# Sample attention in four column groups of TensorE, with plain float32 values

## The chip, the cores and the metric

The kernel runs on one core of a Trainium2 chip. The metric is the device time of one execution in microseconds (us). TensorE is PE in the profile (PEld are its weight loads), VectorE is DVE, ScalarE is ACT, GpSimd is POOL, and SP is the queue that issues the weight transfers.

## The reference

One layer of a hybrid decoder works on a prompt of 1024 tokens and on 8 samples of 4 new tokens each. It has a big input projection, a convolution branch with a LayerNorm, a state-space (S5) branch, dilated attention, an output projection and a feed-forward block. The change lies in the attention of the samples:

```python
kcat = concatenate([k_buf, k_new]);  vcat = concatenate([v_buf, v_new])
idx = L + j - kk * dil                      # 129 keys of each pattern
s = einsum('bthc,btkhc->bhtk', q, kcat[:, idx]) * ATT_SCALE + bias
mx = max(s);  p = exp(s - mx);  den = sum(p)
o = einsum('bhtk,btkhc->bthc', p, vcat[:, idx]) / den;  lse = mx + log(den)
att = sum(softmax(stack(lse over the 3 patterns)) * stack(o))
```

There are 3 patterns of 4 heads of 64. Weighting the three outputs by their denominators is the same as one softmax over the keys of all three patterns, and so the kernel treats them.

## The kernel before, in words

The main line is a list of atoms (`Atom`, run by `run`): dense matmuls `z<-hh,whi` and the like, each f32 product made of three float32r products of high and low halves (`gemm`), 24 matmuls of 128x352 for one chunk of one weight tile. Beside it side generators emit their instructions into the same engine queues: `Side.advance` counts the cost of each atom down, and a generator goes on when its last `yield` is used up. So the numbers after `yield` (`YL`, `YA` to `YD` at the top of the file) set where in each engine's order a step stands. PE, ACT, DVE and POOL work through their orders one instruction after the other.

While the gate projections run (`gate_jobs(GS, 0)`), two generators live beside them: `ln_gen` (L1555 to L1604), the LayerNorm of the convolution branch in three chunks, and `sample_gen` (L946 to L1083), the attention of the samples. `sample_gen` goes like this:

1. Queries go into `Qz`, 32 columns for each pattern, head pair p and sample, zero but for their own place (a memset and 24 copies, L956 and L969), and into `Qa` for the new keys.
2. Scores. `load_k` (L952, POOL) brings the 896 cached keys of one sample, 128x1792, into one of three buffers `kc`. In four bursts, one for each two samples, three key ranges (512, 128 and 256 keys) get four matmuls each: two samples by two head pairs. All four add into the same 32 rows of the score tile, `rows = slice(b2 * 32, b2 * 32 + 32)`. A row stands for sample, head and token.
3. `Qa` against the new keys, the table of biases (L993, L995), exp on ACT (L1016), division on DVE (L1019): tile `Ss`.
4. Ten transposes of `Ss` on PE (L1028, L1039); the 7 tiles of cached keys are split into high and low float32r halves (`PTs`, ACT L1032 and DVE).
5. Values. `load_v` (L1002) uses the buffers of `kc` again. `split_v` makes a high half on ACT (`vh`, L1010) and a low half on DVE (`vl`), in 16 half samples u; each of 56 tiles of 128 keys takes two matmuls into `so[0:32]`.
6. After each two samples ACT copies the sums (`Av`, L1061), four PE transposes turn them (L1067), and at the end the new values are added (`nw`, `asm`) and stored for the branch's projection.

A row block of 32 of a PSUM tile is fed by 32 of the 128 columns of PE's array; such a block is called a column group here. Helpers hide the lines: `mm` records all matmuls as L309 and `TT` all tensor_tensor as L312.

Of the kernel before, what the change touches and what calls it, by code (L numbers as in the profile page):

```python
# [8 lines left out]
F32 = mybir.dt.float32  # L9
# [43 lines left out]
C_ID, C_ONE = 0, 128  # L53
NCST = 256

# [201 lines left out]
def program(tc, I, O):  # L257
# [688 lines left out]
    def sample_gen():  # L946
# [6 lines left out]

        Qz = sa.tile([128, 1792], F32, tag="qp", name="Qz")[:, 0:1536]
        Qz = Qz.rearrange("p (g t b x) -> p g t b x", g=3, t=2, b=8)
        dve.memset(Qz, 0.0)  # L956
        for b in range(3):
# [3 lines left out]
        for g in range(3):  # L961
            for p in range(2):
                for h in range(2):
                    for par in range(2):
                        hp_ = slice(h * 64, h * 64 + 64)
                        c0 = par * 16 + (2 * p + h) * 4
                        dst = Qz[hp_, g, p].rearrange("p (b2 two) x -> p b2 two x", two=2)[:, :, par, c0:c0 + 4]
# [10 lines left out]
        for b2 in range(4):  # L978
            rows = slice(b2 * 32, b2 * 32 + 32)
            for g, c0, n in QK:  # L980
                o = sA[rows, 0:512] if g == 1 else sB[rows, c0 - 512:c0 - 512 + n]
# [15 lines left out]
        vts = {}  # L997
        vhs, vls = {}, {}
# [5 lines left out]
        def split_v(u):  # L1004
            if u < 16:
                b, ks = u // 2, slice(0, 4) if u % 2 == 0 else slice(4, 7)
                n = ks.stop - ks.start
                vhs[u] = sa.tile([128, 4, 256], F32R, tag="vh", name="vh", bufs=2)
                vls[u] = sa.tile([128, 4, 256], F32R, tag="vl", name="vl", bufs=2)
# [10 lines left out]
        yield YB  # L1020

        PTs = sa.tile([128, 7, 8, 2, 16], F32R, tag="qp", name="PTs")
        for half in range(2):
# [5 lines left out]
            for i in range(n):  # L1029
                sv = s[:, i * 128:(i + 1) * 128].rearrange("p (b x) -> p b x", b=8)  # L1030
                ph, pl = [PTs[:, half * 4 + i, :, w, :] for w in range(2)]
# [8 lines left out]
        act.activation(out=PTn.rearrange("p k x -> p (k x)"), in_=s[0:32, 0:384], func=AF.Copy)  # L1040
        split_v(0)
        split_v(1)
        yield 3.0
        Av = sa.tile([128, 1024], F32, tag="Ss", name="Av")
        sT = st()
        for u in range(16):
            b, k0 = u // 2, 4 * (u % 2)
            n = 4 - u % 2
            if u % 4 == 0:
                so = st()  # L1050
            cb = (b % 2) * 256
            for kt in range(n):
                w = PTs[:, k0 + kt].rearrange("p b w x -> p b (w x)")[:, b]
                mm(so[0:32, cb:cb + 256], w, vhs[u][:, kt], u % 2 == 0 and kt == 0, False)
                mm(so[0:32, cb:cb + 256], w, vls[u][:, kt], False, u % 2 == 1 and kt == n - 1)
            split_v(u + 2)
            if u % 2 and b + 3 < 8:
                load_v(b + 3)
            if u % 4 == 3:
                av = Av[0:32, (u // 4) % 2 * 512:(u // 4) % 2 * 512 + 512]  # L1060
                act.activation(out=av, in_=so[0:32, :], func=AF.Copy)  # L1061
            yield YD
            if u % 4 == 3:
                for b2 in range(2):
                    for p in range(2):
                        c0 = p * 256 + (b - 1 + b2) * 32
# [8 lines left out]
        for p in range(2):  # L1075
            for h in range(2):
                hp_ = slice(h * 64, h * 64 + 64)
                c0 = (2 * p + h) * 4
                o = asm[hp_, p, :].rearrange("p (b j) -> p b j", b=8)
                sv = sT[hp_, p * 256:(p + 1) * 256].rearrange("p (b x) -> p b x", b=8)  # L1080
# [1347 lines left out]
```

## Time and profile before

| | us |
|---|---|
| median of 3 runs (1953.93 to 1955.24) | 1955.16 |
| the profiled execution's own time | 1954.96 |
| its span, first to last instruction | 1953.2 |
| PE busy in the span | 1865.4 |
| DVE busy | 1328.9 |
| ACT busy | 727.0 |
| POOL busy | 230.7 |

The profile is one execution. A row of its groups gives an operation with its shape, how often it ran, its busy time and mean length, and the idle time of its engine just before it with what ended that. A plain float32 matmul (weights and values not float32r) leaves two records in the trace, so 48 matmuls of the scores are 96 records. A matmul's record runs on while the next has begun, so its cost in a stream is the distance from start to start.

### The profile page before, as it was taken

The page shows a single profiled execution, that of the slowest core. Times are in us where ns is not written, and L with a number is a line of the kernel's source. Part 1 is how long each engine was busy: PE and PEld are TensorE (multiplying, and loading weights), DVE is VectorE, ACT ScalarE, POOL GpSimd, SP SyncE. Part 2 cuts the span into 40 slices and gives each one's busy share as a digit, 9 for nine tenths or more (in the row PEclk, how much of TensorE's full clock was granted, in tenths as well). Part 3 has the DMA queues.
Part 4 walks back from the last instruction along what each step waited for, and adds up shares of the span by engine and source line. Part 5 has one row for each costly group of instructions (what it writes and reads, how often), then busy time and mean ns, then how long its engine had stood idle before and what let it go on. Part 6 is the DMA issues. An engine that isn't in the chain of part 4 may idle for free. (4 is left out here: it accounts for less than half of the span.)

```text
span 1953.2 us, 33675 instructions
## 1 busy us (share of the span) xinstructions
PE 1865.4 (96%) x13524; PEld 1747.0 (89%) x13524; DVE 1328.9 (68%) x2734; ACT 727.0 (37%) x1430; POOL 230.7 (12%) x386
## 2 busy tenths in 40 slices
PE   7999999899999899999899999999999999999995
PEld 2899799689787789999799999989999999999995
DVE  4777686366366667675596667777777777666695
ACT  3422432432432444222233445434333333374361
POOL 0000001001001013222200001100000000110024
PEclk9999999999999999999899999999999999999997
DMA  7333233233338444233842345542333223576663
GB/s 287 100 102 102 64 109 121 90 107 113 123 123 299 175 163 142 94 118 107 248 144 88 114 149 198 209 160 76 114 107 98 94 83 114 180 245 231 205 211 112
DMA packets 87550, 279.41 MB, mean 143 GB/s; under 512 B 15809, under 2 KB 21537, under 8 KB 85217
## 3 DMA queue, kind: packets, MB, share of 16 engines
q1 hardware_dynamic: 50096, 135.61, 21.7%
q0 software_dynamic: 29952, 115.17, 16.9%
q10 hardware_dynamic: 7344, 26.47, 4.0%
q8 instruction: 106, 1.74, 0.4%
q14 instruction: 52, 0.42, 0.1%
HBM read 209.98 MB, written 68.15 MB: 142 GB/s over the span
## 5 line engine op out<-in xcount | busy, mean ns | idle before, releaser
L309 PE MATMUL z<-hh,whi 128*128 128x352 f32 x1152 | 381.1, 331 | 2.8 <-ACT hh L649 1.5
L309 PE MATMUL z<-hh,wlo 128*128 128x352 f32 x1152 | 374.6, 325 | 3.1 <-DVE wlo L417 3.1
L309 PE MATMUL z<-hl,whi 128*128 128x352 f32 x1152 | 374.1, 325 | 0.8 <-DVE hl L312 0.8
L309 PE MATMUL z<-mh,wop 128*128 128x264 f32 x1916 | 369.4, 284 | 5.4 <-DVE wop L2055 3.0
L309 PE MATMUL z<-ml,wop 128*128 128x264 f32 x1300 | 317.6, 284 | 0.1
L309 PEld LDWEIGHTS z<-mh,wop 128*128 128x128 f32 x1916 | 305.4, 188 | 6.6 <-DVE wop L2055 3.8
L417 DVE SCALAR_TENSOR_TENSOR wlo<-raw,whi 128x1024 fp32r<-128x1024 f32 x132 | 160.9, 1222 | 131.9 <-ACT whi L416 125.1
L309 PEld LDWEIGHTS z<-hh,whi 128*128 128x128 f32 x1152 | 219.9, 191 | 13.9 <-issue 6.2
L309 PEld LDWEIGHTS z<-ml,wop 128*128 128x128 f32 x1300 | 224.1, 188 | 0.3 <-DVE ml L312 0.3
L309 PEld LDWEIGHTS z<-hh,wlo 128*128 128x128 f32 x1152 | 219.8, 191 | 3.7 <-DVE wlo L417 3.7
L309 PEld LDWEIGHTS z<-hl,whi 128*128 128x128 f32 x1152 | 220.1, 191 | 2.4 <-DVE hl L312 1.3
L416 ACT ACTIVATE whi<-raw 128x1024 fp32r<-128x1024 f32 x132 | 139.3, 1056 | 181.8 <-PE z L309 159.9
L1536 DVE SCALAR_TENSOR_TENSOR ycv<-cub,vecs,ycv 128x1024 f32<-128x1024 f32 x120 | 153.9, 1282 | 3.1
L2051 ACT ACTIVATE wop<-raw 128x512 fp32r<-128x512 f32 x132 | 80.7, 619 | 129.5 <-PE z L309 117.0
L309 PE MATMUL z<-xa,wop 128*128 128x264 f32 x768 | 103.7, 284 | 0.0
L309 PEld LDWEIGHTS z<-xa,wop 128*128 128x128 f32 x768 | 97.1, 188 | 0.1
L312 DVE TENSOR_TENSOR wop<-raw,wop 128x512 fp32r<-128x512 f32 x90 | 61.9, 689 | 44.5 <-ACT wop L2051 44.4
L309 PE MATMUL z<-mh,whi 128*128 128x264 f32 x288 | 85.8, 298 | 0.8 <-DVE ft L312 0.6
L309 PE MATMUL z<-ml,whi 128*128 128x264 f32 x288 | 83.3, 289 | 0.0
L309 PE MATMUL z<-mh,wlo 128*128 128x264 f32 x288 | 83.1, 289 | 0.0
L309 PE MATMUL z<-zh,whi 128*128 128x264 f32 x256 | 73.7, 288 | 0.0
L831 ACT ACTIVATE P<-P,stt 128x128 f32<-128x128 f32 (+1 forms) x96 | 42.1, 440 | 83.6 <-DVE stt L828 83.6
(462 smaller groups left out, 3780.2 us busy)
## 6 DMA issues: line engine op xcount, KB each, us to landing
raw<-i_win SPq DMA_DIRECT2D x48, 512.0 KB, 3.8
raw<-i_wfi SPq DMA_DIRECT2D x43, 512.0 KB, 4.0
raw<-i_wfo SPq DMA_DIRECT2D x72, 256.0 KB, 3.5
fd<-ft POOLq DMA_DIRECT2D x22, 792.0 KB, 6.8
raw<-i_wmod SPq DMA_DIRECT2D x32, 512.0 KB, 4.5
gd<-g ACTq DMA_DIRECT2D x24, 528.0 KB, 2.9
g<-gd ACTq DMA_DIRECT2D x24, 528.0 KB, 4.6
ml<-fd POOLq DMA_DIRECT2D x20, 528.0 KB, 6.6
```

What stands on the lines that cost most here:

```text
L309: return pe.matmul(out=out, lhsT=lhsT, rhs=rhs, start=start, stop=stop, **kw)
L312: dve.tensor_tensor(out=out, in0=a, in1=b, op=op)
L416: act.activation(out=hi[:, 0:n], in_=raw[:, 0:n], func=AF.Copy, scale=scale)
L417: dve.scalar_tensor_tensor(out=lo[:, 0:n], in0=raw[:, 0:n], scalar=scale, in1=hi[:, 0:n].bitcast(F32), op0=ALU.mult, op1=ALU.subtract)
L831: act.activation(out=P[:, h, 0:nk], in_=P[:, h, 0:nk], func=AF.Exp, scale=-1.0, bias=stt[:, b, hd:hd + 1], accum_out=stt[:, b, 4 + hd:5 + hd])
L1536: dve.scalar_tensor_tensor(out=a_, in0=ub[:, k:k + TP], scalar=wv[:, k:k + 1], in1=a_, op0=ALU.mult, op1=ALU.add)
L2051: act.activation(out=w[:, 0:n], in_=src, func=AF.Copy, scale=scale)
```

## The change

The scores get their rows in another order: head pair, then parity of the sample, then its number. Each of the four matmuls of two samples then has 32 rows of its own, and the four pairs of samples add into them. The key tiles of a sample's values go over four column groups too, as plain float32 products with unsplit values: four tiles at once, then three. The four partial sums are added while they are turned, by a product with a 128x16 matrix of ones and zeros (`C_FOLD`) in place of the transposes. The yields are new: 72 dense matmuls instead of 24 stand between the softmax and its transposes, a turn stands two steps behind the products it takes, and the LayerNorm's steps stand elsewhere among the dense work.

```diff
-YL = (5.0, 4.0, 4.28, 5.58)
-YA, YB, YC, YD = 4.443, 4.8, 3.45, 1.884
+YL = (5.0, 4.2, 3.8, 4.6)
+YA, YB, YC, YD, YE = 4.443, 11.0, 3.6, 2.3, 4.0
...
+    for r in range(128):
+        if r % 32 < 16:
+            cst[r, C_FOLD + r % 16] = 1.0
...
-                r = b * 16 + h * 4 + j
+                r = h // 2 * 64 + b % 2 * 32 + b // 2 * 8 + h % 2 * 4 + j
...
+        Qf = sa.tile([128, 1920], F32, tag="qp", name="Qz")
+        dve.memset(Qf, 0.0)
...
+        pool.memset(Qa, 0.0)
         for g in range(3):
-            v = Qz[:, g].rearrange("p t (b2 two) x -> p t b2 two x", two=2)
-            TT(Qa[:, g].rearrange("p t (b2 x) -> p t b2 x", b2=4), v[:, :, :, 0], v[:, :, :, 1], ALU.add)
+            for p in range(2):
+                for par in range(2):
+                    c0 = p * 64 + par * 32
+                    dve.tensor_copy(out=Qa[:, g, p, c0:c0 + 32].rearrange("p (b2 x) -> p b2 x", x=8),
+                                    in_=diag(Qz[:, g, p, par, :], slice(0, 8)))
...
-                for par in range(2):
-                    for p in range(2):
-                        mm(o, Qz[:, g, p, 2 * b2 + par, :], kts[2 * b2 + par][:, p, c0:c0 + n],
-                           par == 0 and p == 0, par == 1 and p == 1)
+                for p in range(2):
+                    for par in range(2):
+                        rows = slice(p * 64 + par * 32, p * 64 + par * 32 + 32)
+                        o = sA[rows, 0:512] if g == 1 else sB[rows, c0 - 512:c0 - 512 + n]
+                        mm(o, Qz[:, g, p, par, b2 * 32:b2 * 32 + 32], kts[2 * b2 + par][:, p, c0:c0 + n],
+                           b2 == 0 and g < 2, b2 == 3, skip_group_check=g != 1)
...
-                act.activation(out=vhs[u][:, 0:n], in_=vts[b][:, ks], func=AF.Copy)
-                TT(vls[u][:, 0:n], vts[b][:, ks], vhs[u][:, 0:n].bitcast(F32), ALU.subtract)
...
-                act.activation(out=ph, in_=sv, func=AF.Copy)
-                TT(pl, sv, ph.bitcast(F32), ALU.subtract)
+                if i % 2:
+                    dve.tensor_copy(out=dst, in_=sv)
+                else:
+                    act.activation(out=dst, in_=sv, func=AF.Copy)
...
-                mm(so[0:32, cb:cb + 256], w, vhs[u][:, kt], u % 2 == 0 and kt == 0, False)
-                mm(so[0:32, cb:cb + 256], w, vls[u][:, kt], False, u % 2 == 1 and kt == n - 1)
+            for k0, n in ((0, 4), (4, 3)):
+                for kt in range(n):
+                    c0 = (k0 + kt) * 128 + bi * 16
+                    mm(so[32 * kt:32 * kt + 32, cb:cb + 256], PTf[:, c0:c0 + 32], vts[b][:, k0 + kt], k0 == 0, k0 == 4 or kt == 3)
...
-                        pe.transpose(out=sT[:, c0:c0 + 32], in_=av[:, b2 * 256 + p * 128:b2 * 256 + (p + 1) * 128],
-                                     identity=ident[0:32, 0:32])
+                    mm(sT[:, c0:c0 + 16], av[:, b2 * 256 + p * 128:b2 * 256 + (p + 1) * 128],
+                       cst[:, C_FOLD:C_FOLD + 16], True, True)
...
-                TT(o, An[hp_, p].rearrange("p (b x) -> p b x", b=8)[:, :, c0:c0 + 4], sv[:, :, c0:c0 + 4], ALU.add)
-                TT(o, o, sv[:, :, 16 + c0:20 + c0], ALU.add)
+                TT(o, nv[:, :, :, 4 * h:4 * h + 4], sv[:, :, :, c0:c0 + 4], ALU.add)
```

In the changed file the helper lines are L313 and L316. DVE, at the end of the softmax (`WK` are small S5 steps, `lny` and `lsq` are `ln_gen`). Before:

```order
L312 TENSOR_TENSOR WK<-WK,t_12_5192 128x16 x2
L312 TENSOR_TENSOR PTs<-s,PTs 128x8x16 x7
L312 TENSOR_TENSOR vl<-vc,vh 128x1024
L312 TENSOR_TENSOR vl<-vc,vh 128x768
L1603 SCALAR_TENSOR_TENSOR lny<-lsq,lny 128x1408
L312 TENSOR_TENSOR lny<-lny,lsm 128x1408
L312 TENSOR_TENSOR lsq<-lsq 128x704
L312 TENSOR_TENSOR lsq<-lsq 128x352
```

Now:

```order
L316 TENSOR_TENSOR WK<-WK,t_12_5192 128x16 x2
L1618 SCALAR_TENSOR_TENSOR lny<-lsq,lny 128x1408
L316 TENSOR_TENSOR lny<-lny,lsm 128x1408
L316 TENSOR_TENSOR lsq<-lsq 128x704
L316 TENSOR_TENSOR lsq<-lsq 128x352
```

The splits in front of the LayerNorm's steps are gone, so `lny<-lsq,lny` follows the S5 steps at once. PE, in the values (`lsq` is the LayerNorm's sum of squares). Before, one of the four turns:

```order
L309 MATMUL z<-hh,wlo 128x352
L1067 MATMUL s<-cst,Av 128x32 x4
L309 MATMUL s<-vh,PTs 32x256
L309 MATMUL s<-vl,PTs 32x256
L309 MATMUL s<-vh,PTs 32x256
```

Now, the first of them:

```order
L313 MATMUL z<-hh,wlo 128x352
L313 MATMUL s<-cst,lsq 88x1 x4
L313 MATMUL s<-vc,PTs 32x256 x7
L313 MATMUL s<-cst,Av 128x16 x4
L313 MATMUL s<-vc,PTs 32x256 x7
L313 MATMUL z<-hh,whi 128x352
```

A turn now stands behind the products of the next sample. POOL, which issues the loads of keys (`kc`), values (`vc`) and the LayerNorm's input (`lny<-ycd`). Before:

```order
L952 DMA kc<-i_kc 128x1792 x3
L960 DMA Ss<-i_smp 128x992
L952 DMA kc<-i_kc 128x1792 x5
L1002 DMA vc<-i_vc 128x1792 x3
L1604 DMA cva<-lny 128x4x352
L1555 DMA lny<-ycd 128x4x352
L1002 DMA vc<-i_vc 128x1792 x4
```

Now:

```order
L956 DMA kc<-i_kc 128x1792 x3
L971 DMA Ss<-i_smp 128x992
L981 MEMSET Qa 128x768
L956 DMA kc<-i_kc 128x1792 x5
L1016 DMA vc<-i_vc 128x1792 x3
L1619 DMA cva<-lny 128x4x352
L1570 DMA lny<-ycd 128x4x352
L1027 MEMSET PTs 128x16
L1016 DMA vc<-i_vc 128x1792 x2
```

The loads keep their order; two memsets stand between them.

## Rows read from the trace of the kernel before

**Rows 1.** The page: span, and busy time, share and instructions of each engine.
```profile
span 1953.2 us, 33675 instructions
PE 1865.4 (96%) x13524; PEld 1747.0 (89%) x13524; DVE 1328.9 (68%) x2734; ACT 727.0 (37%) x1430; POOL 230.7 (12%) x386
```

**Rows 2.** Windows: us, busy of PE, PEld, DVE, ACT, POOL (instructions), clock, DMA, GB/s.
```profile
602.00:719.00 117.00, 105.39 (x613) 83.12 (x613) 69.27 (x198) 46.65 (x73) 10.69 (x20) 0.97 0.52 187
654.00:690.00 36.00, 29.75 (x182) 26.74 (x181) 24.23 (x51) 19.57 (x32) 3.68 (x6) 0.91 0.54 188
```

**Rows 3.** Groups on PE, 602 to 719 us: records | busy us, mean ns | idle before.
```profile
L309 PE MATMUL s<-vh,PTs 128*32 128x256 f32 x56 | 14.9, 296 | 3.4 <-ACT vh L1010 3.4
L309 PE MATMUL s<-vl,PTs 128*32 128x256 f32 x56 | 14.8, 298 | 3.4 <-DVE vl L312 3.2
L309 PE MATMUL s<-kc,Qz 128*32 128x512 f32 x32 | 14.7, 596 | 0.4 <-DMA kc<-i_kc 0.4
L309 PE MATMUL s<-kc,Qz 128*32 128x256 f32 x32 | 7.6, 379 | 0.0
L309 PE MATMUL s<-cst,lsq 128*88 128x1 f32 x24 | 2.2, 213 | 1.4 <-DVE lsq L312 1.4
L1067 PE MATMUL s<-cst,Av 32*128 32x32 f32 x16 | 1.7, 227 | 0.7 <-ACT Av L1061 0.7
L1028 PE MATMUL s<-cst,Ss 128*128 128x128 f32 x7 | 1.0, 276 | 2.4 <-DVE Ss L1019 2.4
```

**Rows 4.** Timeline of PE, the second burst of the scores: start us, length us.
```profile
613.02 6.22 PE L309 MATMUL s<-kc,Qz 128*32 128x512 f32 x24
619.17 0.43 PE L309 MATMUL z<-hh,whi 128*128 128x352 f32 x1
```

**Rows 5.** Timeline of PEld in the same burst.
```profile
613.47 0.11 PEld L309 LDWEIGHTS s<-kc,Qz 128*32 128x32 f32 x1 [0.32 <-issue]
613.90 0.11 PEld L309 LDWEIGHTS s<-kc,Qz 128*32 128x32 f32 x1 [0.32 <-issue]
```

**Rows 6.** Timeline of PE in the S5 branch: 32 records in two column groups.
```profile
752.61 2.18 PE L309 MATMUL s<-U,Gin 128*64 128x144 f32 x32
754.73 0.43 PE L309 MATMUL z<-hh,whi 128*128 128x352 f32 x1
```

**Rows 7.** The tile kc: its transfers; timeline of PE in the first burst.
```profile
DMA to landing us min/median/max: 4.8/6.2/18.9
...
604.57 0.62 PE L309 MATMUL s<-kc,Qz 128*32 128x512 f32 x1 [0.44 <-DMA kc<-i_kc]
```

**Rows 8.** Timeline of PE behind the last burst.
```profile
640.67 0.43 PE L309 MATMUL z<-hh,whi 128*128 128x352 f32 x1
...
644.59 0.76 PE L309 MATMUL s<-rs_dg,cst 88*128 88x352 f32 x2
...
645.78 1.42 PE L309 MATMUL s<-ks__87,Qa 128*128 128x32 f32 x12
647.03 0.41 PE L309 MATMUL z<-hh,whi 128*128 128x352 f32 x1
```

**Rows 9.** Timeline of PE, one half of two samples' values, 14 records, and one turn.
```profile
699.26 0.28 PE L309 MATMUL s<-vh,PTs 128*32 128x256 f32 x1
...
700.90 0.32 PE L309 MATMUL z<-hh,whi 128*128 128x352 f32 x1
...
705.42 0.43 PE L1067 MATMUL s<-cst,Av 32*128 32x32 f32 x4
705.78 0.30 PE L309 MATMUL s<-vh,PTs 128*32 128x256 f32 x1
```

**Rows 10.** Timeline: the LayerNorm's second chunk, DVE and then PE.
```profile
655.95 0.28 DVE L312 TENSOR_TENSOR PTs<-s,PTs 128x128 fp32r<-128x128 f32 x1
...
662.63 1.62 DVE L1603 SCALAR_TENSOR_TENSOR lny<-lsq,lny 128x1408 f32<-128x1408 f32 x1
...
668.83 0.76 PE L309 MATMUL s<-cst,lsq 128*88 128x1 f32 x8 [1.40 <-DVE lsq L312]
```

More of the change, by code (lines that the diff above doesn't have):

```diff
@@ L53 @@
 C_ID, C_ONE = 0, 128
-NCST = 256
+C_FOLD = 256
+NCST = C_FOLD + 16
 def _tiles(w, kt, n):
@@ L952, in load_k, with diag @@
             pool.dma_start(out=kts[b], in_=I['kc'][b])
-        Qz = sa.tile([128, 1792], F32, tag="qp", name="Qz")[:, 0:1536]
-        Qz = Qz.rearrange("p (g t b x) -> p g t b x", g=3, t=2, b=8)
-        dve.memset(Qz, 0.0)
+        Qf = sa.tile([128, 1920], F32, tag="qp", name="Qz")
+        Qz = Qf.rearrange("p (g t two x) -> p g t two x", g=3, t=2, two=2)
+        def diag(v, n):
+            return v.rearrange("p (b2 y) -> p b2 y", y=40)[:, :, n]
+        dve.memset(Qf, 0.0)
         for b in range(3):
@@ L965, in sample_gen @@
                         hp_ = slice(h * 64, h * 64 + 64)
-                        c0 = par * 16 + (2 * p + h) * 4
-                        dst = Qz[hp_, g, p].rearrange("p (b2 two) x -> p b2 two x", two=2)[:, :, par, c0:c0 + 4]
+                        dst = diag(Qz[hp_, g, p, par, :], slice(4 * h, 4 * h + 4))
                         src = qs[hp_, g, p, :].rearrange("p (b2 two j) -> p b2 two j", two=2, j=4)[:, :, par, :]
@@ L978, in sample_gen @@
         for b2 in range(4):
-            rows = slice(b2 * 32, b2 * 32 + 32)
             for g, c0, n in QK:
-                o = sA[rows, 0:512] if g == 1 else sB[rows, c0 - 512:c0 - 512 + n]
-                for par in range(2):
-                    for p in range(2):
-                        mm(o, Qz[:, g, p, 2 * b2 + par, :], kts[2 * b2 + par][:, p, c0:c0 + n],
-                           par == 0 and p == 0, par == 1 and p == 1)
+                for p in range(2):
[4 more added lines that the diff above has]
+                           b2 == 0 and g < 2, b2 == 3, skip_group_check=g != 1)
             for b in (2 * b2 + 3, 2 * b2 + 4):
@@ L997, in sample_gen @@
         vts = {}
-        vhs, vls = {}, {}
         def load_v(b):
@@ L1002, in load_v @@
             pool.dma_start(out=vts[b], in_=I['vc'][b])
[L1004 to L1009, printed above, removed]
-                act.activation(out=vhs[u][:, 0:n], in_=vts[b][:, ks], func=AF.Copy)
-                TT(vls[u][:, 0:n], vts[b][:, ks], vhs[u][:, 0:n].bitcast(F32), ALU.subtract)
         for b in range(3):
@@ L1020, in sample_gen @@
         yield YB
-        PTs = sa.tile([128, 7, 8, 2, 16], F32R, tag="qp", name="PTs")
+        PTf = sa.tile([128, 1920], F32, tag="qp", name="PTs")
+        pool.memset(PTf[:, 896:912], 0.0)
+        PTs = PTf[:, 0:896].rearrange("p (k b x) -> p k b x", k=7, b=8)
         for half in range(2):
@@ L1029, in sample_gen @@
             for i in range(n):
-                sv = s[:, i * 128:(i + 1) * 128].rearrange("p (b x) -> p b x", b=8)
-                ph, pl = [PTs[:, half * 4 + i, :, w, :] for w in range(2)]
-                act.activation(out=ph, in_=sv, func=AF.Copy)
-                TT(pl, sv, ph.bitcast(F32), ALU.subtract)
+                sv = s[:, i * 128:(i + 1) * 128].rearrange("q (p b x) -> q b p x", p=2, b=8)
+                dst = PTs[:, half * 4 + i].rearrange("q b (p x) -> q b p x", p=2)
+                if i % 2:
+                    dve.tensor_copy(out=dst, in_=sv)
+                else:
+                    act.activation(out=dst, in_=sv, func=AF.Copy)
         nw = sa.tile([128, 768], F32, tag="qa", name="nw")
@@ L1045, in sample_gen, with turn @@
         sT = st()
[L1046 to L1049, printed above, removed]
+        sums = []
+        def turn(b, av):
+            for b2 in range(2):
+                for p in range(2):
+                    c0 = p * 128 + (b - 1 + b2) * 16
+                    mm(sT[:, c0:c0 + 16], av[:, b2 * 256 + p * 128:b2 * 256 + (p + 1) * 128],
+                       cst[:, C_FOLD:C_FOLD + 16], True, True)
+        for b in range(8):
+            if b % 2 == 0:
                 so = st()
             cb = (b % 2) * 256
-            for kt in range(n):
-                w = PTs[:, k0 + kt].rearrange("p b w x -> p b (w x)")[:, b]
-                mm(so[0:32, cb:cb + 256], w, vhs[u][:, kt], u % 2 == 0 and kt == 0, False)
-                mm(so[0:32, cb:cb + 256], w, vls[u][:, kt], False, u % 2 == 1 and kt == n - 1)
-            split_v(u + 2)
-            if u % 2 and b + 3 < 8:
+            bi = b % 2 * 4 + b // 2
+            for k0, n in ((0, 4), (4, 3)):
+                for kt in range(n):
+                    c0 = (k0 + kt) * 128 + bi * 16
+                    mm(so[32 * kt:32 * kt + 32, cb:cb + 256], PTf[:, c0:c0 + 32], vts[b][:, k0 + kt], k0 == 0, k0 == 4 or kt == 3)
+            if b + 3 < 8:
                 load_v(b + 3)
-            if u % 4 == 3:
-                av = Av[0:32, (u // 4) % 2 * 512:(u // 4) % 2 * 512 + 512]
-                act.activation(out=av, in_=so[0:32, :], func=AF.Copy)
+            if b % 2:
+                av = Av[:, b // 2 % 2 * 512:b // 2 % 2 * 512 + 512]
+                act.activation(out=av, in_=so, func=AF.Copy)
+                sums.append((b, av))
             yield YD
[L1063 to L1066, printed above, removed]
-                        pe.transpose(out=sT[:, c0:c0 + 32], in_=av[:, b2 * 256 + p * 128:b2 * 256 + (p + 1) * 128],
-                                     identity=ident[0:32, 0:32])
+            if b % 2 and b > 1:
+                turn(*sums.pop(0))
+        yield YE
+        turn(*sums.pop(0))
         s = st()
@@ L1078, in sample_gen @@
                 c0 = (2 * p + h) * 4
-                o = asm[hp_, p, :].rearrange("p (b j) -> p b j", b=8)
-                sv = sT[hp_, p * 256:(p + 1) * 256].rearrange("p (b x) -> p b x", b=8)
-                TT(o, An[hp_, p].rearrange("p (b x) -> p b x", b=8)[:, :, c0:c0 + 4], sv[:, :, c0:c0 + 4], ALU.add)
-                TT(o, o, sv[:, :, 16 + c0:20 + c0], ALU.add)
+                o = asm[hp_, p, :].rearrange("q (b2 par j) -> q par b2 j", par=2, j=4)
+                sv = sT[hp_, p * 128:(p + 1) * 128].rearrange("q (b2 par x) -> q par b2 x", par=2, x=16)
+                nv = An[hp_, p, p * 64:p * 64 + 64].rearrange("q (par b2 x) -> q par b2 x", par=2, x=8)
+                TT(o, nv[:, :, :, 4 * h:4 * h + 4], sv[:, :, :, c0:c0 + 4], ALU.add)
         pool.dma_start(out=attd[:, :, TP:T].rearrange("t p x -> p t x"), in_=asm)
```

2 lines of the change are left out of this document (removed).

## The prediction

> **What bounds the kernel now.** I read the page first. PE is busy 96% of the span and no other engine is near that [rows 1], so what the change takes from PE's stream, or from its waits, comes off the time, and what it takes from DVE and ACT counts only where PE waits for them. Next comes the window over the stage that is changed, from the first burst of scores (602 us) to the end of the sample's attention (719 us): there PE is busy 105.4 of 117 us and its clock is 0.97 [rows 2]. So some 11.6 us are idle, and the groups of PE say on whom: 3.4 us on the high halves of the values (ACT), 3.4 on their low halves (DVE), 2.4 on the softmax (DVE), 1.4 on the LayerNorm (DVE), 0.7 on a copy of sums (ACT) and 0.4 on a key load [rows 3]. In the middle of this, from 654 to 690 us, the granted clock is 0.91 of full [rows 2]: 9% of 36 us missing at half rate (1.2 instead of 2.4 GHz) is a stretch of 6.5 us, in which 3.2 us of work were lost; it lies among these waits. Last I read the timeline, for what a burst costs from its start to the start of the next dense matmul.
>
> **The scores.** A burst of 24 records takes 613.02 to 619.17, 6.15 us [rows 4]: 7168 columns, 0.86 ns each, one record after the other, since all write the same 32 rows. In the change four in a row write four column groups. That groups overlap is seen with two of them: the 32 records of 144 columns of the S5 branch would take 3.95 us at 0.86 ns a column, and took 2.12, that is half (1.98) and 0.14 at the ends [rows 6]. Four groups are shown nowhere. The bounds are a quarter of 6.15 with nothing lost (1.5 us) and no overlap (6.15); I take 1.7, a quarter and 0.15, since two groups share the array all but perfectly and plain float32 is the same there.
>
> The loads now set the pace. The first burst cannot go on before the second sample's keys, which PE saw at 604.57 [rows 7]; before, the first sample's matmuls ran until then, now the second matmul of the burst waits for them. It ends at 604.6 + 1.7 = 606.3. Each later burst needs a tile whose buffer the burst before gave back; such a load takes at least 4.8 us to land, 6.2 in the median [rows 7], where the 24 dense matmuls between take 3.9 (640.67 to 644.59, [rows 8]). The first of two loads is the one that is needed first, so I take 4.9 with its issue, a pace of 4.9 + 1.7 = 6.6, and the last burst ends at 606.3 + 3 x 6.6 = 626.1. It ended at 640.67 [rows 8]. **Scores: -14.6 us**, of which the waits for keys eat 3 to 5.
>
> **The values.** Half of two samples, 14 records, takes 699.26 to 700.90, 1.64 us [rows 9]; there are 8, 13.1 us. Now a sample has 14 records of 256 plain float32 columns, the fullest group four of them: 1024 columns at 0.86 ns is 0.88, with 0.15 at the ends 1.03, for 8 samples 8.2. Bounds: 7.0 without ends, 24.6 without overlap. **-4.9 us.** It is four times the columns' work of float32r at a quarter of the time, so here the gain is small and hangs wholly on the four groups.
>
> **The turns.** Four transposes took 705.42 to 705.78, 0.36 us, four times 1.4 [rows 9]. The product with the fold matrix is plain float32, two records each with 128 weight columns; the nearest row is `Qa`, 12 such records in 645.78 to 647.03, 0.104 each [rows 8]. Eight are 0.83, with ends 1.0, four times 4.0. Bounds 1.4 and 5. **+2.6 us.**
>
> **The waits.** Those on the halves of values (6.8), the copy of sums (0.7, now two steps ahead) and the softmax (2.4, now 72 dense matmuls, 11.7 us, ahead) go; the LayerNorm is late next. In the trace DVE is through with the S5 steps behind the softmax at 655.95, 11.4 us after the matmul `rs_dg` at 644.59 [rows 8, 10]; that run of steps is the same in the change, and now `lny<-lsq,lny` follows. From there to the matmul `lsq` took 662.63 to 668.83, 6.2 us [rows 10], all of it a chain of DVE, ACT and DVE. So `lsq` can run 17.6 us after `rs_dg`. PE will have, in between, 2.4 us to the next dense matmul [rows 8] and 72 dense ones, 11.7: 14.1. It waits 3.5 us. At the third chunk the chain is the same without the softmax in it, with some 12 us of PE's work beside it; I take 0.6, between 0 and the 3.5 of the second. New waits 4.1 against 11.3 (without the 0.4 that belongs to the scores): **-7.2 us.** An idle time is counted from the modelled end of a record, 0.16 past the slot it costs (a dense record lasts 0.32 and the next begins 0.16 later), so each of ten waits cost 0.16 more and two will: **-1.3 us.**
>
> **The clock.** Half of the 6.5 us at 1.2 GHz should go with half of the waits: **-1.6 us**, bounds 0 and -3.2.
>
> **At no cost.** The longer memset of `Qz` and the copies of `Qa` make DVE later by about a microsecond, an estimate; the keys that come only at 604.57 [rows 7] cover it, 2.4 us past the first burst's start, and without that cover it would cost that microsecond. POOL's two memsets stand ahead of loads that wait for buffers anyhow; SP's queue is not touched. ACT and DVE lose 16 splits of values each, which shows only in the waits above. The LayerNorm's last input is loaded on POOL behind the result of its first chunk, which comes no later against PE than the waits above say; if it is late, that is the rival on the waits.
>
> **Sum.** -14.6 - 4.9 + 2.6 - 7.2 - 1.3 - 1.6 = -27.0 us. The profiled execution took 1954.96, so 1928.0; the median of the runs is 0.2 above it: **1928.2 us**.
>
> **Rivals.**
> - *Two at a time.* The array takes two groups together but not four; only two are shown [rows 6]. A burst is 3.2 us, the four end 1.5 x 4 = 6.0 later; the values take 1.75 a sample, 14.0, 5.8 more. 1940.0. For it: nothing else is shown. Against it: two lose only 0.14 us.
> - *The loads of weights stand free.* In the trace a load of 32 columns takes 0.11 us and the loads start every 0.43, the length of one record (613.47, 613.90), while the 24 records fill their burst without a hole [rows 4, 5]: a load lies under the matmul before it, with the same 128 rows. So I add nothing. The Trainium skill, "TensorE: Matmul & The Clock Gate", section "What overlaps and what doesn't", says that a weight load overlaps with matmuls in flight only when their row groups differ, and these four all use all rows. By that rule the trace should show the loads as holes, which it doesn't. As a mechanism of this kernel: should the four loads of a round, run together, each time hold up the array for 0.11 us [rows 5], then 6 rounds in 4 bursts and 4 rounds in 8 samples, 56, cost 6.2 us: 1934.4.
> - *The waits return.* PE's work shrinks faster than what feeds it: loads of keys land in the median 6.2 instead of 4.8 (3 x 1.4), the LayerNorm's third chunk waits 3.5 instead of 0.6, and the clock gives nothing back: 4.2 + 2.9 + 1.6 = 8.7, 1936.9. For it: every idle row names ACT or DVE [rows 3]; against it: their queues get lighter.
> - *One after the other*, the change not doing what it says, and slower. Groups of 32 columns with all rows take turns, as the score matmuls did in one group. The scores stay at 6.15; the values become 112 records of 256 columns, 24.6 us instead of 13.1, +11.5; the turns +2.6; only the waits on the halves go, 6.8 us and seven times 0.16, 7.9 in all. 11.5 + 2.6 - 7.9 = +6.2, 1961.2. It decides where the groups overlap less than 1.14 times: then 24.6 us of scores, 24.6 of values and 2.6 of turns no longer fit into the 24.6 + 13.1 + 7.9 that they replace. Against it stand the S5 rows with 1.87 times [rows 6].
>
> **How the numbers follow.** Forecast 0.73, weight loads 0.06, waits 0.09, two at a time 0.08, one after the other 0.04. The low end is the forecast without ends on bursts and samples (-2), with the clock's other half (-1.6), with loads at 4.8 and keys never late (-3): 1921.5. The high end takes in weight loads, waits and two at a time with a microsecond: 1941. Outside lie the last rival and some of the bounds. A difference under 0.2% (4 us) cannot be told from none here. Every case but one is well past it: faster 0.94, same 0.02, slower 0.04.
>
> **What would show it.** Right: in the profile after, score records that start in fours a few ns apart, a burst of about 1.7 us, PE waiting for the DMA of `kc` in several bursts; value groups of 1 us; no `vh` or `vl`; one wait of 3 to 4 us on DVE ahead of `lsq`; the stage about 27 us shorter and the stretches before and behind it as long as they were. Wrong: bursts of 3 us (pairs) or of 6 (turns), waits on ACT's `PTs` or `Av`, or the time found in a later stage.

## The result and the profile after

The changed kernel took **1934.58 us** in the median (1932.45 to 1937.01, 4 runs) against 1955.2 us before (1953.93 to 1960.94, 4 runs): 0.9895 of the time before, 95% interval 0.9881 to 0.9908. That is 20.6 us gained, where 27.0 were forecast (1928.2 us). Faster, inside the range (1921.5 to 1941.0), and 6.4 us short of the predicted number. The profiled execution has a span of 1932.9 us against 1953.2 [rows 1], 20.3 less.

The page of the changed kernel:

```profile
span 1932.9 us, 33662 instructions
...
PE 1848.1 (96%) x13540; PEld 1736.1 (90%) x13540; DVE 1311.6 (68%) x2719; ACT 713.2 (37%) x1411; POOL 231.3 (12%) x388
```

The stage in windows: from the first burst of scores to the first `rs_dg` (the program's order puts it behind the fourth burst), from there to the LayerNorm's third `lsq`, from there to the end of the stage; the last line is the stretch right behind the wait for the second `lsq`. Columns as in [rows 2].

```profile
603.50:635.30 31.80, 27.49 (x203) 20.45 (x203) 21.65 (x113) 4.52 (x7) 4.23 (x8) 1.00 0.83 310
635.30:674.40 39.10, 35.25 (x226) 31.64 (x225) 22.86 (x49) 17.96 (x30) 4.03 (x7) 0.91 0.54 189
674.40:698.80 24.40, 24.37 (x201) 20.09 (x201) 8.11 (x18) 9.86 (x16) 2.55 (x6) 1.00 0.54 183
...
652.80:659.60 6.80, 6.75 (x30) 6.59 (x31) 4.27 (x18) 0.72 (x3) 0.88 (x2) 0.50 0.36 106
```

The three add up to 95.3 us; before, the same work went from 602.22 to 718.89, 116.7 us. The stage gave 21.4 us. It begins 1.3 us later than before (603.5 against 602.2), although PE has the same 3674 matmul records up to there. In the eight runs below of which that holds too, the first burst starts anywhere from 601.4 to 604.5 us, in the second run of the changed kernel at 603.2; so the 1.3 us are put down to scatter between executions, and the stage is what there is to explain.

The groups of PE in the stage, which answer to [rows 3]:

```profile
L313 PE MATMUL s<-vc,PTs 128*32 128x256 f32 x112 | 8.3, 385 | 0.0
L313 PE MATMUL s<-kc,Qz 128*32 128x512 f32 x32 | 8.0, 604 | 4.3 <-DMA kc<-i_kc 2.6 <-DVE t L316 1.7
L313 PE MATMUL s<-kc,Qz 128*32 128x256 f32 x32 | 4.8, 379 | 0.0
L313 PE MATMUL s<-cst,Av 128*128 128x16 f32 x32 | 4.0, 258 | 0.0
...
L313 PE MATMUL s<-cst,lsq 128*88 128x1 f32 x24 | 2.8, 237 | 3.9 <-DVE lsq L316 3.9
```

No value, turn or softmax transpose waits any more. Two waits are left: 4.3 us on keys and 3.9 us on the LayerNorm's `lsq`. (The 1.7 us put down to the DVE tile `t` stand ahead of the first burst's second sample, whose key load lands at 606.17, 0.13 us before the burst goes on; in the run with five buffers the same wait is named as the key load, so it is taken for that here.) Note what the busy time does with overlapping records: 112 value records of 385 ns would be 43 us one after the other, and are 8.3.

The timeline of PE over the first and the third burst:

```profile
603.51 1.04 PE L313 MATMUL s<-kc,Qz 128*32 128x512 f32 x2
606.30 1.71 PE L313 MATMUL s<-kc,Qz 128*32 128x512 f32 x22 [1.75 <-DVE t L316]
607.94 0.43 PE L313 MATMUL z<-hh,whi 128*128 128x352 f32 x1
...
619.65 1.05 PE L313 MATMUL s<-kc,Qz 128*32 128x512 f32 x2
622.94 1.71 PE L313 MATMUL s<-kc,Qz 128*32 128x512 f32 x22 [2.24 <-DMA kc<-i_kc]
624.58 0.43 PE L313 MATMUL z<-hh,whi 128*128 128x352 f32 x1
```

Two records of the first sample run, then the burst stands until the second sample's keys are there, and the other 22 are through in 1.64 us (606.30 to 607.94, and again 622.94 to 624.58). So four column groups do run together. But the third burst took 4.93 us (619.65 to 624.58), 3.3 of them waiting. Why, the loads show. The first fence has the issues from 613 to 616 us after the change, the second those from 614 to 616 us and the one from 618 to 620 us before it (queue, count, KB, us to landing):

```profile
kc<-i_kc POOLq DMA_DIRECT2D x1, 896.0 KB, 7.5
gd<-g ACTq DMA_DIRECT2D x1, 528.0 KB, 4.1
raw<-i_win SPq DMA_DIRECT2D x1, 512.0 KB, 4.7
```

```profile
gd<-g ACTq DMA_DIRECT2D x1, 528.0 KB, 2.9
raw<-i_win SPq DMA_DIRECT2D x1, 512.0 KB, 3.7
...
kc<-i_kc POOLq DMA_DIRECT2D x1, 896.0 KB, 4.8
```

Before, the store of `g` landed at 617.3 and the load of weights at 619.0, so the key load, issued at 618.67, shared only 0.3 us with them. Now the burst ends earlier against them: the key load goes out at 615.37, the load of weights lands 3.6 us later, and all three take longer; the one that PE waits for takes 7.5 us.

The wait of the second `lsq`, then two samples' values and a turn between them:

```profile
652.85 1.30 PE L313 MATMUL s<-cst,lsq 128*88 128x1 f32 x8 [3.27 <-DVE lsq L316]
...
682.71 1.06 PE L313 MATMUL s<-vc,PTs 128*32 128x256 f32 x14
683.70 1.06 PE L313 MATMUL s<-cst,Av 128*128 128x16 f32 x8
684.69 1.06 PE L313 MATMUL s<-vc,PTs 128*32 128x256 f32 x14
```

0.99 us a sample (682.71 to 683.70) and 0.99 a turn, against 1.64 a half of two samples and 0.36 a turn in [rows 9]. The second `lsq` comes 17.55 us behind `rs_dg` (635.30 to 652.85).

### The profile page after: what moved, and what is told of

Same layout as the page of the kernel before. It is cut to its first block, busy times and chain, and to the rows that moved or that the text cites. A ratio compares the mean times of both kernels' runs of the same rounds, so it can differ in the third digit from the quotient of the medians.

```text
span 1932.9 us, 33662 instructions
## 1 busy us (share of the span) xinstructions
PE 1848.1 (96%) x13540; PEld 1736.1 (90%) x13540; DVE 1311.6 (68%) x2719; ACT 713.2 (37%) x1411; POOL 231.3 (12%) x388
## 5 line engine op out<-in xcount | busy, mean ns | idle before, releaser
L313 PE MATMUL z<-hh,whi 128*128 128x352 f32 x1152 | 380.7, 331 | 2.7 <-ACT hh L653 1.5
L313 PE MATMUL z<-hh,wlo 128*128 128x352 f32 x1152 | 373.6, 324 | 3.1 <-DVE wlo L421 3.1
L313 PE MATMUL z<-mh,wop 128*128 128x264 f32 x1916 | 370.6, 285 | 4.2 <-ACT wop L2066 2.2
L313 PE MATMUL z<-hl,whi 128*128 128x352 f32 x1152 | 373.0, 324 | 0.8 <-DVE hl L316 0.8
L313 PE MATMUL z<-ml,wop 128*128 128x264 f32 x1300 | 317.2, 284 | 0.2 <-DVE ml L316 0.2
L313 PEld LDWEIGHTS z<-mh,wop 128*128 128x128 f32 x1916 | 305.5, 189 | 5.0 <-DVE wop L2070 2.5
L313 PEld LDWEIGHTS z<-hh,whi 128*128 128x128 f32 x1152 | 219.1, 190 | 15.8 <-issue 7.9
L313 PEld LDWEIGHTS z<-ml,wop 128*128 128x128 f32 x1300 | 224.4, 188 | 0.4 <-DVE ml L316 0.4
L313 PEld LDWEIGHTS z<-hh,wlo 128*128 128x128 f32 x1152 | 218.8, 190 | 3.7 <-DVE wlo L421 3.7
L313 PEld LDWEIGHTS z<-hl,whi 128*128 128x128 f32 x1152 | 219.3, 190 | 2.4 <-DVE hl L316 1.4
L313 PE MATMUL z<-xa,wop 128*128 128x264 f32 x768 | 105.9, 287 | 0.0
L313 PEld LDWEIGHTS z<-xa,wop 128*128 128x128 f32 x768 | 99.6, 192 | 0.1
L316 DVE TENSOR_TENSOR wop<-raw,wop 128x512 fp32r<-128x512 f32 x90 | 61.8, 688 | 44.8 <-ACT wop L2066 44.8
L313 PE MATMUL z<-mh,whi 128*128 128x264 f32 x288 | 85.7, 298 | 1.1 <-DVE ft L316 0.6
L313 PE MATMUL z<-ml,whi 128*128 128x264 f32 x288 | 83.1, 289 | 0.0
L313 PE MATMUL z<-mh,wlo 128*128 128x264 f32 x288 | 83.0, 288 | 0.0
L313 PE MATMUL z<-zh,whi 128*128 128x264 f32 x256 | 73.6, 288 | 0.0
L313 PE MATMUL z<-zl,whi 128*128 128x264 f32 x256 | 72.8, 284 | 0.0
```

The costliest lines, as they stand in the source:

```text
L313: return pe.matmul(out=out, lhsT=lhsT, rhs=rhs, start=start, stop=stop, **kw)
L316: dve.tensor_tensor(out=out, in0=a, in1=b, op=op)
```

## The experiments

Ten runs followed, one of them of the changed kernel again, in three groups; each group shared its runs of the kernel before (medians 1956.12, 1958.05 and 1955.72 us). As these differ by up to 2.3 us, and from the 1955.2 above by up to 2.9, runs of different groups are compared by their ratios; "by the ratio" means the ratio times 1955.2.

| run | median us | ratio to before | 95% interval |
|---|---|---|---|
| the change | 1934.58 | 0.9895 | 0.9881 to 0.9908 |
| scores_only | 1944.0 | 0.9939 | 0.9927 to 0.9952 |
| values_only | 1945.34 | 0.9954 | 0.9937 to 0.9970 |
| five_bufs | 1935.06 | 0.9895 | 0.9881 to 0.9908 |
| lsq_later | 1935.34 | 0.9896 | 0.9883 to 0.9910 |
| by_group | 1942.7 | 0.9922 | 0.9905 to 0.9939 |
| second_later | 1927.87 | 0.9856 | 0.9836 to 0.9876 |
| both | 1929.48 | 0.9852 | 0.9835 to 0.9870 |
| both_first_later | 1925.74 | 0.9836 | 0.9821 to 0.9851 |
| after_again | 1935.37 | 0.9895 | 0.9878 to 0.9912 |
| first_second_later | 1934.05 | 0.9890 | 0.9873 to 0.9907 |

**Where did the missing 6 us go: scores or values?** `scores_only` is the kernel before with the scores' part of the diff (four row groups, the row order of mask and `Qa`); the values stay split, at the old yields. `values_only` is the kernel before with the other part, its yields included.

> The kernel before with the scores alone in four column groups; values, their halves, their yields and turns as before. Theory 1 (the scores are worth what the traces of the change show, and no more because key loads set their pace): four bursts take about 14.6 us instead of 25.2 from their starts to the next dense matmul, so 10.6 us off 1955.2: 1944.6 us, with key loads of 7 us landing behind a store and a weight load that are in flight with them. Theory 2 (the scores are worth the 14.6 us that the prediction gave them, and the 6 us were lost at the values): 1940.6 us. Theory 3 (what the scores give is taken back by the waits on the halves of the values and on the softmax, which now come earlier against the engines that feed them): 1949 us or more, with the vh, vl or Ss waits grown by some 4 us.

> The kernel before with the values alone in four column groups (turns, yields and the LayerNorm's places as in the change); the scores in 32 rows of one group as before. Theory 1: the change less its scores, 20.6 - 10.6 = 10 us off: 1945 us; value groups of 1.0 us a sample, turns of 0.9, a wait of 3 us and more ahead of lsq that brings a stretch at half rate with it. Theory 2 (the loss of 6 us lies here): 6 us off, 1949 us. Prediction's own terms for this part (-4.9 + 2.6 - 7.2 - 1.3 - 1.6): 1942.8 us.

The scores alone gave 11.9 us (0.0061 of 1956, interval 9.4 to 14.3) where the prediction had 14.6; the values alone 9.0 (5.9 to 12.3) where it had 12.4 with waits and clock. The two add up to the whole, 20.9 against 20.6. The 6 us of theory 2 lie at the edge of the interval of `values_only`; the traces decide. The stage is 106.3 us in `scores_only` (602.59 to 708.91) and 106.7 in `values_only` (602.29 to 708.97), 10.4 and 10.0 less than before, as theory 1 has it. The key load behind the second burst, in `scores_only` (issued between 614 and 616 us):

```profile
kc<-i_kc POOLq DMA_DIRECT2D x1, 896.0 KB, 7.5
```

Again 7.5 us, with the old values behind it: the loss belongs to the scores and their loads, not to what the values do to them.

**Take the waits away, one at a time.** The halves of values left room for two more buffers:

```diff
-    kts[b] = sa.tile([128, 2, 896], F32, tag="kc", name="kc", bufs=3)
+    kts[b] = sa.tile([128, 2, 896], F32, tag="kc", name="kc", bufs=5)
...
-            for b in (2 * b2 + 3, 2 * b2 + 4):
+            for b in (2 * b2 + 5, 2 * b2 + 6):
```

(values likewise, and the fourth and fifth load at the start, behind the mask), and the LayerNorm's second sums of squares later:

```diff
-            yield YL[1]
+            yield YL[1] + (3.9 if c == 1 else 0.0)
```

> The change with five buffers instead of three for the tiles of keys and values, in the room that the halves of the values left; the matmuls' order is the same. Theory 1 (key loads set the pace of the bursts): the waits for keys in bursts 2 to 4 go, 3.00 + 4.93 + 2.23 become three times 1.75, 4.9 us off 1934.6: 1929.7 us; the first burst waits as before. Theory 3 (whatever the bursts save, the chain of the LayerNorm and the softmax on DVE takes back, since it is the bound of the stage): the keys' waits go and the wait ahead of lsq grows from 3.3 to about 8 us, 1934.6 us. Slower by a microsecond or two if two more loads at the start delay the first ones.

> The change with the sums of squares of the LayerNorm's second chunk 24 dense matmuls later in the program, everything else the same. Theory 1: the wait of 3.3 us ahead of lsq goes, and with it the stretch at 1.2 GHz behind it (0.5 + 1.0 + 1.6 = 3.1 us lost there): 6.4 us off 1934.6, 1928.2 us, or 1931.3 if the stretch at half rate comes all the same. Rival: the wait only moves, to the transposes of the softmax or to the third chunk, whose chain now begins 4 us later: 1934.6 us.

Neither moved the time (0.9895 and 0.9896 of before, as the change itself). Here the windows are needed, since each did in its own place what theory 1 said. Five buffers, the same three pieces as above:

```profile
601.40:629.10 27.70, 25.83 (x203) 19.70 (x203) 21.17 (x110) 4.53 (x7) 4.22 (x8) 1.00 1.01 414
629.10:668.30 39.20, 33.75 (x227) 30.17 (x225) 23.38 (x53) 17.96 (x30) 4.23 (x9) 0.96 0.55 196
668.30:697.30 29.00, 29.00 (x200) 23.33 (x200) 8.20 (x18) 9.88 (x16) 1.31 (x2) 0.82 0.27 89
```

The bursts' piece fell from 31.8 to 27.7 us: bursts 3 and 4 wait for nothing. The middle piece kept its length to 0.1 us, 39.2 against 39.1, though the clock in it rose from 0.91 to 0.96: what the clock lost less there, PE stood waiting more. In the second run of the change, in `values_only` and in `by_group`, which have the same LayerNorm yields, it is 39.2, 39.1 and 39.1 us. The waits of PE in this run say for whom:

```profile
PE s L313 <- DVE lsq L316: 5.4, 2, 3.3
PE s L313 <- DMA kc<-i_kc: 1.9, 2, 1.5
```

5.4 us instead of 3.9. So from `rs_dg` to the third `lsq` the LayerNorm's chain over DVE and ACT sets the length, and what PE does in it is hidden. The last piece is then 4.6 us longer with the same records and no wait: its clock is 0.82, that is 18% of 29 us or 5.2 us missing at 1.2 GHz, right behind the wait of 2.2 us for the third `lsq`. Theory 1 was right on the keys and theory 3 on the sum, though in this trace what was taken back came by way of the clock behind a wait, not by 8 us of waiting.

The later sums of squares, from the first burst, and then the 25 us behind the stage; last, the change at that place in its first and in its second run:

```profile
603.80:636.80 33.00, 28.50 (x203) 20.86 (x203) 21.40 (x111) 4.53 (x7) 4.23 (x8) 0.95 0.80 299
636.80:676.90 40.10, 39.01 (x288) 34.58 (x286) 24.02 (x52) 19.75 (x33) 5.28 (x11) 1.00 0.60 216
676.90:694.70 17.80, 17.35 (x142) 14.48 (x140) 7.19 (x18) 7.71 (x13) 1.04 (x2) 1.00 0.40 141
694.70:720.00 25.30, 23.85 (x131) 22.78 (x131) 19.30 (x69) 8.07 (x13) 10.49 (x23) 0.87 0.77 238
```

```profile
698.80:724.10 25.30, 25.30 (x161) 24.45 (x160) 21.83 (x73) 8.78 (x14) 10.23 (x22) 1.00 0.66 222
...
699.10:724.40 25.30, 25.30 (x152) 24.54 (x152) 21.81 (x73) 8.78 (x14) 10.24 (x22) 0.93 0.66 221
```

No wait for `lsq` is left, and the clock stays full over the middle piece; the stage is 90.9 us, 4.4 less than in the change. Then 25 us behind it run at 0.87 (3.3 us missing) with 1.4 us idle, all of it for `GT`, a tile that DVE makes for the S5 branch. Only a part of that belongs to the edit. Half of what is missing lies at the start of these 25 us, and there the unaltered kernel has the same in its second run (0.93, with no wait) and nothing in its first. The other half begins behind the wait for `GT` (at 715.9), a wait that neither trace of the change has. So 3.1 of the 4.4 us came back by way of the next chain on DVE, 1.4 as waiting and 1.7 as a low clock behind it. The rest can't be told from scatter: from the stage's end to the last instruction the change took 1234.2 us in one trace and 1237.4 in the other, this run 1240.9. The rival's number came true by another way than the rival's.

**Does the pace or the company make the key load slow?** `second_later` leaves three buffers and puts 24 dense matmuls more ahead of the second burst:

```diff
-            yield YC
+            yield YC + (3.9 if b2 == 0 else 0.0)
```

> The change with 24 dense matmuls more between the first burst of scores and the second; everything behind keeps its distance. Theory (the key load that the third burst needs took 7.5 us because a store of 528 KB and a weight load of 512 KB were in flight with it): its issue now lies behind their landing, it takes 5.5 us or less, the third burst waits under 1 us instead of 3.3, the second not at all instead of 1.4; bursts of 11 us in sum instead of 14.6, so up to 3.6 us off 1934.6 if nothing behind takes it back: 1931.0. Rival (loads at this pace take 7 us in any case, since two are always in flight): 7 us and more again, a third burst with a wait near 3 us, 1933.3.

The load that the third burst needs, issued between 616 and 617 us; the third burst:

```profile
kc<-i_kc POOLq DMA_DIRECT2D x1, 896.0 KB, 4.7
```

```profile
620.35 2.28 PE L313 MATMUL s<-kc,Qz 128*32 128x512 f32 x24
```

4.7 us instead of 7.5, a burst of 2.2 us up to the next dense matmul instead of 4.9, and the second without a wait. The company it is; the other traces agree. Where the weight load landed 3.5 to 4.9 us behind the issue of this key load (the change, its second run, `scores_only`, `lsq_later`), the key load took 7.4 to 8.0 us; 2.4 us behind it (`by_group`), 6.9; 1.1 us behind it, here, 4.7; 0.3 us behind it, in the kernel before, 4.8. In all of them the next key load, of the same size, was issued some 2 us behind it, so two in flight are not enough. The store and the weight load now share their time mostly with a key load that nobody waits for, and took 5.9 and 5.2 us. 1927.87 us, 0.9856 of before (0.9836 to 0.9876): 6.7 us better than the change (7.6 by the ratios), for one number and no memory. The stage is 6.0 us shorter (89.3 us, 601.4 to 690.7, against 95.3). The bursts gave 4.8 (4.3, 1.65, 2.2 and 1.65 us instead of 4.4, 3.0, 4.9 and 2.2). The waits on `lsq` fell from 3.9 to 0.7 us, as the scores now stand later against the LayerNorm, and 1.7 us less are missing at 1.2 GHz; a new wait of 2.1 us on `g` (ACT) and some 1.4 us more at the transposes and the first values stand against that.

**What makes four groups run together?** The same matmuls, each group's own behind each other:

```diff
-            for g, c0, n in QK:
-                for p in range(2):
-                    for par in range(2):
+            for p in range(2):
+                for par in range(2):
+                    for g, c0, n in QK:
```

> The change with the twelve score matmuls of a burst in another order: all that write one column group behind each other, then the next group, instead of four groups in turn. Theory (matmuls are started in the program's order, so only neighbours in it that write different column groups run together): a burst becomes 5.5 to 6.2 us again (overlap only where one group follows another), the last one ends some 10 us later, 1944.5 us. Rival (each column group has work of its own that runs whenever its weights and data are there, whatever the order): bursts of 1.65 us without waits, 1934.6 us.

```profile
614.74 4.36 PE L313 MATMUL s<-kc,Qz 128*32 128x512 f32 x24
619.03 0.43 PE L313 MATMUL z<-hh,whi 128*128 128x352 f32 x1
```

4.29 us (614.74 to 619.03): between both theories, and neither is right. The records under way from 615.63 to 615.72 show why:

```profile
L313 PE MATMUL s<-kc,Qz x3: 273/592/617, 615.2 to 615.6; 128*32 128x512 f32 x2, 128*32 128x128 f32 x1
```

A group has two records each of 512, 128 and 256 columns, in this order. Its first 512-column record began at 614.74 and is over, its second and its first 128-column one are under way, and beside them is a third 512-column record, which can only be the next group's. It started together with the first 128-column record, ahead of the second and of both 256-column ones, three records that stand ahead of it in the program. So work of a later group does pass, but in these records no more than two groups run at a time. The Trainium skill, "TensorE: Matmul & The Clock Gate", section "What overlaps and what doesn't", has matmuls start strictly in the program's order; this trace shows otherwise for different column groups. The time, 1942.7 us, is 5.3 us above the change by the ratios, and the stage in the trace is 5.4 longer (100.6 us): the order in turn is worth that, with the same columns.

**Together, and earlier keys.** `both` has the five buffers and the later sums of squares; `both_first_later` also a first burst 24 dense matmuls later (`yield YA + 3.9`).

> Five buffers and the later sums of squares together, since either alone gave nothing. Theory 1 (two bounds stand behind each other: the key loads ahead of the first rs_dg, the chain of the LayerNorm behind it, each hiding what the other gives back): 27.7 us from the first burst to rs_dg as with five buffers, 40.0 to the third lsq and 17.8 to the end as with the later sums, 85.5 us instead of 95.3, 9.7 off 1934.6: 1925 us. Rival (the stage's waits are not what counts: what goes from them comes back as stretches at half rate behind the stage, some 4 us): 1929 us or more; if the chain of DVE and ACT is the bound of the stage, 1934.6.

> The same with the first burst 24 dense matmuls later in the program, so that its keys are there: its 4.2 us become 1.7, the second burst's wait of 1.4 goes, and the second chunk's sums of squares stand 96 dense matmuls behind rs_dg instead of 72. Theory 1: another 3.9 us off what both give, some 1921 us. Rival: the softmax, which begins 4 us later against the dense matmuls, lets the values' loads or the LayerNorm's third chunk be late: as both, 1925 us or more.

`both`, the three pieces and the 26 us behind them:

```profile
604.30:632.00 27.70, 25.83 (x204) 19.75 (x204) 21.21 (x110) 4.54 (x7) 4.24 (x8) 1.00 1.01 414
632.00:671.90 39.90, 38.93 (x286) 34.49 (x285) 24.06 (x54) 19.79 (x33) 4.25 (x9) 1.00 0.58 210
671.90:689.20 17.30, 17.30 (x141) 14.44 (x139) 7.33 (x18) 7.76 (x13) 1.02 (x2) 1.00 0.22 68
689.20:715.00 25.80, 23.35 (x130) 22.25 (x130) 20.33 (x70) 8.09 (x13) 10.60 (x23) 0.87 0.78 243
```

27.7, 39.9 and 17.3 us: theory 1's pieces to half a microsecond, 84.9 in all. Then come 2.5 us of waits on `GT`,

```profile
PE s L1355 <- DVE GT L316: 2.5, 2, 1.3
```

and a clock of 0.87 again, with the stretch at 1.2 GHz beginning in the second of these waits (at 708.3). One bound of the LayerNorm gone, the next chain on DVE ends last, and part of the 10.3 us that the stage gave comes back there. 1929.48 us looks like the rival's number, but the kernel before took 2.9 us more in this group than in the first runs: by the ratio it is 1926 (1923 to 1930), and the time does not tell theory 1 from its rival.

`both_first_later` has the lowest median, 1925.74 us, 0.9836 of before (0.9821 to 0.9851), faster than both kernels of this case; the intervals of `both` and `second_later` overlap its own. By the ratio it is 1923 us. It lies 3.7 below `both`, where theory 1 had 3.9, but not for theory 1's reason. Its stage is 84.7 us with 24 dense matmuls (3.9 us) fewer in it, so the same work took longer: new waits of 3.3 us for `g` (ACT) and 1.7 for `lsq`, and 3.4 us missing at 1.2 GHz, took back what the bursts gave. The gain stands behind the stage, where `GT` is waited for 0.4 us instead of 2.5 and the clock is full. Its first burst has its keys, and shows what four groups cost when nothing is missing, on PE and on PEld:

```profile
606.45 1.72 PE L313 MATMUL s<-kc,Qz 128*32 128x512 f32 x24
608.10 0.43 PE L313 MATMUL z<-hh,whi 128*128 128x352 f32 x1
```

```profile
606.45 0.16 PEld L313 LDWEIGHTS s<-kc,Qz 128*32 128x32 f32 x8 [0.22 <-DVE t L316]
606.91 0.13 PEld L313 LDWEIGHTS s<-kc,Qz 128*32 128x32 f32 x4 [0.30 <-issue]
607.34 0.35 PEld L313 LDWEIGHTS s<-kc,Qz 128*32 128x32 f32 x12 [0.30 <-issue]
```

1.65 us for the 7168 columns that took 6.15 in one group.

**The change again, and the keys by order alone.** `after_again` is the change unaltered; `first_second_later` has its three buffers, with 24 dense matmuls more ahead of the first burst and 24 ahead of the second.

> The change itself, unaltered, beside the next kernel on one chip: 0.9895 of the kernel before again, some 1935 us, with the same third burst (its key load in flight with a store and a weight load, over 7 us) and the same wait of 3.3 us ahead of lsq. If the start of the program, not the stage, set the 1.3 us by which the first burst began later than before, that burst begins at another time in this run, 601 to 605 us.

> The change with 24 dense matmuls more ahead of the first burst and 24 more between the first and the second, three buffers as in the change. If the key loads are all that the bursts wait for, all four take 1.65 us, 6.6 in sum instead of 14.6 in the change and 9.8 with the second burst alone later: 3 us off 1927.9, some 1925 us. Rival: the stage's values now stand so late in the program that their last groups follow each other without dense matmuls between them, and wait for loads into three buffers; what the bursts gave comes back there, 1928 us or more.

The change gave 0.9895 again, and the load behind its second burst took 8.0 us. `first_second_later` is a miss: 1934.05 us, where 1925 were expected and the rival had 1928 or more. Its keys are nearly all there, and its waits are these:

```profile
PE s L313 <- DVE lsq L316: 6.6, 2, 3.6
PE s L313 <- DMA vc<-i_vc: 1.0, 1, 1.0
PE s L313 <- DMA kc<-i_kc: 0.3, 1, 0.3
```

The rival's loads of values cost 1.0 us; the 6.6 on the LayerNorm, which the move put at other places against the dense matmuls, were in no expectation. Its stage is 90.5 us with 24 dense matmuls (3.9 us) fewer in it, only 0.9 less than in the change for the same work. Moving one stage past 48 dense matmuls moves it against every other chain too.

## Why the prediction was right, and by what it was off

Each term against the trace of the change, in the order of the sum:

| term | predicted | measured in the stage |
|---|---|---|
| scores | -14.6 | -10.6 |
| values | -4.9 | -5.3 |
| turns | +2.6 | +2.3 |
| waits | -7.2 | -7.4 |
| ends of waits | -1.3 | -0.4 (what is left of 21.4) |
| clock | -1.6 | 0.0 |

- **Scores.** That four groups share the array was the bold step, and it held: 1.64 and 1.65 us with the keys there, against the 1.7 taken. The **pace of the loads** failed: "so I take 4.9 with its issue, a pace of 4.9 + 1.7 = 6.6". The bursts ended 607.94, 615.00, 624.58 and 631.38, that is 7.1, 9.6 and 6.8 us apart; 27.9 us from the first start to the last end (603.51 to 631.38) against 38.45 before (602.22 to 640.67), where 23.9 were predicted. 3.0 of the missing 4.0 us are the one load that met a store and a weight load. A time to landing was taken from a stretch in which the loads had little but each other for company, for a stretch in which the change itself put them in company. `second_later`, with 4.7 us for the same load, shows it.
- **Values and turns** were right to 0.4 us. 1.86 for the first two samples and six times 0.99 are 7.8 us, from 13.1; the turns cost 0.81 to 0.99 each, 3.7 in all, from 1.4.
- **Waits.** Those on the halves, on the copy of sums and on the softmax went. The LayerNorm became late next, at the place and of the size that was worked out: 17.55 us from `rs_dg` to `lsq` against 17.6, a wait of 3.27 against 3.5, and 0.60 at the third chunk against 0.6.
- **Clock.** "Half of the 6.5 us at 1.2 GHz should go with half of the waits" failed. Before, two stretches at half rate stood behind waits:

```profile
654.80:658.20 3.40, 3.40 (x14) 3.40 (x13) 2.23 (x14) 1.00 (x4) 0.00 (x0) 0.50 0.83 276
685.50:688.90 3.40, 2.88 (x14) 2.36 (x15) 1.60 (x3) 1.43 (x3) 0.53 (x1) 0.51 0.23 34
```

  Both went with their waits, but the new wait of 3.27 us brought its own, twice as long (652.8 to 659.6, 0.50): 3.4 us missing in either kernel. Most waits went and the loss stayed. It stood in the piece whose length the LayerNorm's chain sets, which kept its length in `five_bufs` with half of that loss, so taking it away there would have given little.
- **Weight loads.** In the trace eight loads of 0.11 us lie within 0.16 us, and a burst loses 0.11 us in all over a quarter of 6.15 (1.54), not 0.11 in each of its six rounds. So the rival by which each round of loads holds up the array for 0.11 us (6.2 us in all), the rule of the Trainium skill that stands beside it ("TensorE: Matmul & The Clock Gate", section "What overlaps and what doesn't") included, does not hold for these column groups. Its number, 1934.4, is 0.2 us from the measured one, and that is chance: the loads of keys and the clock make up the difference, not the loads of weights.
- **The waits return** was the rival that told most: its 4.2 us on the keys came as 4.0, though not as 1.4 three times but as 3.0 once and some tenths each at the others, and the clock gave nothing back, as it said; the wait of 3.5 us at the third chunk did not come. **Two at a time** and **one after the other** are out for the order of the change; `by_group`, at 4.29 us a burst where the first of them has 3.2, comes nearest to it when the order is another.

The two failed steps, the pace of the loads and the clock, are 4.0 and 1.6 us, 5.6 of the 6.4 missing. The other terms miss by under 1 us each and cancel; 0.8 us lie outside the stage.

## What to carry to other kernels

A transfer's time to landing belongs to its company: when work ahead of it shrinks, list what else is in flight at the new moment of its issue before its old time is used again, and move it by a number in the order before giving it memory. When a wait is taken away and the time stays, compare the stretches between fixed points of the program: one of constant length names the chain that bounds it. A low clock right behind a wait can be part of that wait's price, but compare a second trace of the unaltered kernel before a low clock is put down to an edit. Column groups in turn, neighbours in the program, were worth nearly their full number here (3.7 of 4); the same groups behind each other gave 1.4 here (6.15 to 4.29).

## What was not expected of the hardware

- Four matmuls of plain float32 with 32 columns of weights each ran at 3.7 times the speed of one (6.15 to 1.65 us), their loads of weights together as well (eight of 0.11 us in 0.16).
- A matmul for an idle column group started ahead of earlier ones of a busy group (4.29 us a burst in `by_group`, not 6.15).
- A key load of 896 KB took 4.7 to 4.8 us with little but the next key load beside it, and 7.4 to 8.0 with a store and a load of some 500 KB each in flight as well.
- The same kernel does not always show the same clock in the same place: behind the stage it was full for 25 us in the change's first trace and 0.93 in its second, without a wait of PE in either. The wait for keys in the third burst was followed by a stretch at 1.2 GHz in `lsq_later` (2.15 us of waiting, 1.7 us missing) and by none in the change (2.24), its second run (2.72) and `scores_only` (2.23). Why stays open; no run here tells it.
